# The second MLP product of a decoder layer, with the weight operands of two neighbouring sets side by side

## The chip, the cores and the metric

The kernel runs on one core of a Trainium2 chip. It is one launch that computes one layer of a decoder on 512 tokens. What counts is the device time of that launch in microseconds. The time before is 2219.13 us, the median of 3 runs (2218.69 to 2220.06).

The engines of the core go by short names: PE is the matrix engine, with the weight loads of its instructions listed apart as PEld; DVE, ACT and POOL are the vector, scalar and general engines; SP issues transfers. Transfers that SP issues are run by the hardware queue, those that POOL issues by the software queue, and both are carried by the same 16 DMA engines.

## What is computed

```python
def reference(x, w_in, conv_w, a_log, dt_bias, delta_norm_w, attn_sinks, rel_bias,
              w_o, ln1_g, ln1_b, w_up, w_down, ln2_g, ln2_b):
    for l in range(DEPTH):
        mixed = hybrid_mixer(x, w_in[l], conv_w[l], a_log[l], dt_bias[l], delta_norm_w[l],
                             attn_sinks[l], rel_bias, w_o[l])
        x = layer_norm(DN_ALPHA * x + mixed, ln1_g[l], ln1_b[l])
        x = layer_norm(DN_ALPHA * x + squared_relu_mlp(x, w_up[l], w_down[l]), ln2_g[l], ln2_b[l])
    return x

def squared_relu_mlp(h, w_up, w_down):
    a = jax.nn.relu(h @ w_up)
    return (a * a) @ w_down
```

`x` is 512 tokens by 2048, `w_up` 2048 by 8192, `w_down` 8192 by 2048, all float32. The mixer (a banded attention and a gated delta rule side by side) fills the first part of the launch and is not touched by the change. The change is in the last product, `(a * a) @ w_down`.

## The kernel before

**One product out of three.** A float32 operand is cut in two parts, hi and lo: ACT rounds it to the matrix format (hi), DVE subtracts that from the source (lo). A product of two operands is three matrix products summed in PSUM, hi by hi, hi by lo, lo by hi (`mul3`, line 105; `split`, line 109; their instructions stand under lines 107, 110 and 111).

**Seven products out of eight.** The last product is tiled in `g` (8 pieces of 1024 of the contraction) and `j` (4 pieces of 512 output columns). One `(g, j)` is a *set*. Within it, tokens, contraction and columns are each halved, and a scheme of seven products in place of eight is run: product `m` multiplies an operand of the activations (512 of the contraction by 256 tokens, sums of quarters, made by `Rows`) with an operand of the weights (512 of the contraction by 256 columns). The products come in the order `ORDER = (0, 3, 4, 6, 2, 1, 5)`. Results go to three PSUM banks per set, named in `PAIR`: products 0, 2, 1, 5 accumulate in bank "a", 3 in "e", 4 and 6 in "f". After every product DVE adds the bank, as it then stands, into a quarter of the output `y` (which lies in the tile `mix`; line 1002, called here the *evacuation*). So when one bank serves two products in a row, the second may not be written before DVE has read the first.

**The weights come by a chain.** The weight operand of most products is a sum of quarter blocks of `w_down` (512 KB each). The sums are made by transfers: a raw tile is loaded, cut for one product, and then a transfer issued by POOL adds the next block into the same raw tile in place (`accum_op=ALU.add`, line 186). A set has two such tiles. The tile x serves products 0, 4, 2 and 5, with an add after 0, after 4 and after 2. The tile y serves 3, 6 and 1, with a plain load after 3 (SP, line 188) and an add after 6. Before, `chained_pair` runs two neighbouring sets (`j` and `j + 1`) in turn: product `m` of the one, `m` of the other, then the next `m`. A chain of one tile therefore has four cuts from one use to the next.

**What sets the order.** `Stream` (line 113) holds the loads and the cuts in lists. Each `get()` hands out one cut operand and pumps: as far as room is free, loads and cuts are written into the program ahead. There are four slots for cut operands, so the cut that is written at a `get()` goes into the slot that the operand before has just left, and serves the operand three places further on. Each engine works its instructions strictly in the order in which they were laid down, and waits on semaphores of the others. `down` (line 1353) calls `get()`, then lays down 24 matmuls, then the evacuation.

**The activations' operands** of the next `g` are made meanwhile: `Rows` loads `hf` from memory (line 1293), sums quarters on DVE into `st` (line 1002) and cuts them into slots, one step after each of seven of the fourteen products (`steps`, line 1380).

## Time and profile before

| | |
|---|---|
| median of 3 runs | 2219.13 us (2218.69 to 2220.06) |
| the profiled execution's own time | 2220.53 us |
| its span, first to last instruction | 2218.7 us |
| mean granted clock of PE | 0.989 |
| PE busy | 2152.5 us of the span |
| DVE, ACT, POOL busy | 1461.3, 981.7, 327.5 us |
| the last product's stage | from about 1540 to 2208 us of the span |

The page gives busy times for the whole launch, and stages differ; the stage of the last product is read in windows of the trace, counted in microseconds from the span's start. A matmul is pipelined: its own length in the trace is longer than the distance to the next one, so the pace of a stage is its length divided by the number of matmuls in it. A row of the timeline or of a group of instructions names the line, the engine, the operation, the tile written and the tiles read, and then the idle time of that engine ahead of it with what ended that idle time.

### The profile page before, as it was taken

To read this page: it belongs to the slowest core of one execution; us is meant where nothing else is said; L and a number is where in the kernel's file an instruction comes from. 1 tells how busy PE (TensorE), PEld (TensorE's weight loads), DVE (VectorE), ACT (ScalarE), POOL (GpSimd) and SP (SyncE) were. 2 spreads that over 40 slices of the span, in tenths; PEclk is the share of its full clock that TensorE was granted. 3 is DMA by queue.
4 is the path that set the end of the run, shared out by engine and by line. 5 is a ranking of instruction groups with operands and counts; after the bars stand their busy time and mean duration, and the time that the engine had idled before them with its cause. 6 is when DMAs were issued, how large, how long until landed. Compare 5 with 4: busy or idle time off the path is not lost.

```text
span 2218.7 us, 37232 instructions
## 1 busy us (share of the span) xinstructions
PE 2152.5 (97%) x15051; PEld 1974.7 (89%) x15051; DVE 1461.3 (66%) x2170; ACT 981.7 (44%) x1474; POOL 327.5 (15%) x395
## 2 busy tenths in 40 slices
PE   8999999999999999899999999998999999999996
PEld 6777788788888887799999999998999999999995
DVE  3455667566654337867755565667778778778787
ACT  3244434334233224555555555555444444444442
POOL 0122020101100000321111211110111211112113
PEclk9999999999999999999999999999999999999998
DMA  7322341332324231499898898986788888888862
GB/s 208 95 72 81 96 116 58 98 87 69 98 64 170 90 122 46 136 206 232 212 210 216 207 219 208 207 202 225 178 219 215 195 212 216 203 211 213 204 146 93
DMA packets 164392, 352.63 MB, mean 159 GB/s; under 512 B 20123, under 2 KB 92236, under 8 KB 161660
## 3 DMA queue, kind: packets, MB, share of 16 engines
q0 software_dynamic: 38336, 130.08, 32.1%
q1 hardware_dynamic: 125884, 220.18, 29.5%
q8 instruction: 118, 1.93, 0.4%
q14 instruction: 54, 0.44, 0.1%
HBM read 325.01 MB, written 24.66 MB: 158 GB/s over the span
## 4 chain that ended last, share of the span: by engine, by line
PE 75%; issue 8%; DMA 7%; DVE 6%; ACT 2%; POOL 2%; SPq 0%; POOLq 0%; ACTq 0%; DVEq 0%
PE b L107 45%; PE pj L107 16%; PE po L107 8%; DMA raw<-in_w_down_dram 2%; DMA hf<-hd 2%; DVE lo L111 1%; DMA T<-in_w_down_dram 1%; PE ps_s L507 1%; ACT hi L110 1%; DVE mix L1439 1%; PE ps_o L554 1%; DMA g<-in_ln_dram 1%; DMA xc<-in_x_dram 1%; DMA C<-grow 1%; PE ps_pt L538 1%
## 5 line engine op out<-in xcount | busy, mean ns | idle before, releaser
L107 PE MATMUL b<-slot,hi 128*128 128x256 f32 x3584 | 646.7, 283 | 8.7 <-DVE slot L1041 3.3
L111 DVE TENSOR_TENSOR lo<-raw,hi 128x1024 fp32r<-128x1024 f32 x339 | 417.4, 1231 | 315.5 <-ACT hi L110 312.9
L110 ACT ACTIVATE hi<-raw 128x1024 fp32r<-128x1024 f32 x339 | 358.5, 1058 | 502.5 <-PE b L107 251.8
L107 PEld LDWEIGHTS b<-slot,hi 128*128 128x128 f32 x3584 | 555.5, 190 | 10.6 <-DVE slot L1041 4.1
L107 PE MATMUL b<-slot,lo 128*128 128x256 f32 x1792 | 507.3, 283 | 1.6 <-DVE lo L111 1.6
L107 PE MATMUL b<-hi,slot 128*128 128x256 f32 x2608 | 476.2, 282 | 9.6 <-ACT hi L110 9.6
L107 PE MATMUL pj<-slot,hi 128*128 128x512 f32 x1408 | 458.8, 403 | 0.0
L107 PEld LDWEIGHTS b<-hi,slot 128*128 128x128 f32 x2608 | 405.9, 189 | 10.6 <-ACT hi L110 10.6
L107 PE MATMUL b<-lo,slot 128*128 128x256 f32 x1304 | 368.0, 282 | 0.8 <-DVE lo L111 0.7
L107 PEld LDWEIGHTS b<-slot,lo 128*128 128x128 f32 x1792 | 340.2, 190 | 2.5 <-DVE lo L111 2.5
L107 PEld LDWEIGHTS pj<-slot,hi 128*128 128x128 f32 x1408 | 260.2, 189 | 60.6 <-issue 6.9
L107 PE MATMUL pj<-slot,lo 128*128 128x512 f32 x704 | 281.5, 400 | 1.0 <-DVE lo L111 1.0
L110 ACT ACTIVATE hi<-T 128x1024 fp32r<-128x1024 f32 x164 | 173.6, 1059 | 199.8 <-PE b L107 178.6
L111 DVE TENSOR_TENSOR lo<-T,hi 128x1024 fp32r<-128x1024 f32 x164 | 201.7, 1230 | 83.8 <-ACT hi L110 83.6
L107 PEld LDWEIGHTS b<-lo,slot 128*128 128x128 f32 x1304 | 246.3, 189 | 1.4 <-DVE lo L111 1.3
L1002 DVE TENSOR_TENSOR mix<-mix,b 128x512 f32<-128x512 f32 x223 | 152.0, 682 | 61.3 <-PE b L107 61.0
L107 PE MATMUL b<-hl,slot 128*128 128x256 f32 x1296 | 165.8, 284 | 4.8 <-DVE mix L1002 4.8
L107 PEld LDWEIGHTS b<-hl,slot 128*128 128x128 f32 x1296 | 160.0, 192 | 6.2 <-issue 4.3
L107 PEld LDWEIGHTS pj<-slot,lo 128*128 128x128 f32 x704 | 132.9, 189 | 30.4 <-DVE lo L111 1.9
L186 POOL DMA_DIRECT2D raw<-in_w_down_dram x90 | 77.7, 863 | 498.6 <-DVE lo L111 276.7
L1002 DVE TENSOR_TENSOR F<-F,b 128x512 f32<-128x512 f32 x144 | 98.9, 686 | 77.2 <-PE b L107 75.8
L107 PE MATMUL po<-hi,slot 128*128 128x512 f32 x448 | 140.7, 395 | 0.0
(263 smaller groups left out, 2118.9 us busy)
## 6 DMA issues: line engine op xcount, KB each, us to landing
raw<-in_w_down_dram POOLq DMA_DIRECT2D x90, 512.0 KB, 5.7
raw<-in_w_in_dram SPq DMA_DIRECT2D x88, 512.0 KB
raw<-in_w_up_dram POOLq DMA_DIRECT2D x84, 512.0 KB, 6.4
T<-in_w_down_dram SPq DMA_DIRECT2D x60, 512.0 KB
T<-in_w_up_dram SPq DMA_DIRECT2D x56, 512.0 KB
raw<-in_w_up_dram SPq DMA_DIRECT2D x44, 512.0 KB
raw<-in_w_down_dram SPq DMA_DIRECT2D x34, 512.0 KB
raw<-in_w_o_dram SPq DMA_DIRECT2D x32, 512.0 KB
```

The costliest lines, as they stand in the source:

```text
L107: nc.tensor.matmul(ps, a, b, start=first, stop=last, skip_group_check=more)
L110: nc.scalar.activation(hi, src, AF.Copy)
L111: nc.vector.tensor_tensor(out=lo, in0=src, in1=hi.bitcast(F32), op=ALU.subtract)
L186: nc.gpsimd.dma_start(src, nxt_, accum_op=ALU.add)
L507: nc.tensor.matmul(sc, qT[hp, b * P:(b + 1) * P], kd[hp, e, b * P + k0 - 128:(b + 1) * P], start=True, stop=True)
L538: nc.tensor.transpose(pst[:, (bb * 2 + kk) * P:(bb * 2 + kk + 1) * P], lg[a][:, b, kk * P:(kk + 1) * P], ident)
L554: nc.tensor.matmul(pso[a * 64:(a + 1) * 64, b * P:(b + n) * P], vt[:, b, vf_, vh:vh + 64], pTf[:, (2 * b + 1) * P:(2 * b + 1 + n) * P], st ...
L1002: eng.tensor_tensor(out=dst, in0=p, in1=q, op=op)
L1439: nc.vector.tensor_tensor(out=yt, in0=yt, in1=g, op=ALU.mult)
```

## The change

Two neighbouring sets are no longer run in turn but as one. A weight operand now holds the blocks of both sets side by side, so that one matmul has 512 columns. Since a slot for cut operands keeps its size, such an operand is given in two halves of the contraction (`kh` = 0 and 1, 256 each): two `get()`, each with 12 matmuls (2 tiles of 128 tokens, 2 steps of the contraction, 3 parts). A bank now holds one tile of 128 tokens by the 256 columns of both sets, and it is evacuated in the second half, once per tile of tokens (`t`).

The raw tiles of the chains are pairs: one tile holds the block of both sets. There are four pairs; those of the first stage's raw tiles are joined to two, one comes in the pool `fp2`, and one is the tile `F` of the first product once that has ended. The fourth slot for cut operands moves from `F` to `fp2` in turn. The next transfer of a chain is issued after the cut of the second half, as two transfers, one per block. The tiles `st` for sums of the activations become two halves of one fixed slot (`sums`), and the tile `T` becomes a slot for an activations' operand. The very last sets (`g` = 7, `j` = 2 and 3) keep their way.

The raw and cut tiles of the whole launch are now slices of one large tile each (`raws`, `cuts`); up to the last product, the order on each engine stays the same but for a few neighbours that change places.

```diff
--- before.py
+++ after.py
...
-            self.cut_free, self.used = deque(), []
-            self.room(pool, raws, cuts)
-            self.raw_free[tag].extend([(pool, raws)] * raws)
+            self.cut_free, self.used, self.kept = deque(), [], None
+            self.base = pool.tile([P, raws, 1024], F32, name="raws", bufs=1)
+            self.free["raw"].extend(self.base[:, j, :] for j in range(raws))
+            self.n_raw = raws
+            self.room(pool.tile([P, cuts, 2048], F32R, name="cuts", bufs=1))
+
+        def room(self, t):
+
+            self.cut_free.extend(t[:, j, :] for j in range(t.shape[1]))
...
         def load(self, tag):
-            live, loads, room = self.live[tag], self.loads[tag], self.raw_free[tag]
+            live, loads, free = self.live[tag], self.loads[tag], self.free[tag]
             while live and self.last[live[0][0]] < self.n_cut:
-                room.append(live.popleft()[1])
-            if not loads or not room or loads[0][2] > self.n_cut:
+                free.append(live.popleft()[1])
+            if not loads or loads[0][2] > self.n_cut:
+                return False
+
...
                 return False
             key, srcs, _ = loads.popleft()
-            a = srcs[0].shape[1]
-            pool, bufs = tok = room.popleft()
-            raw = pool.tile([P, a, 1024 // a], F32, tag=tag, name=tag, bufs=bufs)
-            n = 1024 // a // len(srcs)
-            for j, src in enumerate(srcs):
-                nc.sync.dma_start(raw[:, :, j * n:(j + 1) * n], src)
+            tok = free.popleft()
+            if tag == "W":
+                raw = tok
+                self.bring(raw, srcs)
+            else:
+                a = srcs[0].shape[1]
+                raw = tok.rearrange("p (a b) -> p a b", a=a)
+                n = 1024 // a // len(srcs)
+                for j, src in enumerate(srcs):
+                    nc.sync.dma_start(raw[:, :, j * n:(j + 1) * n], src)
             self.raws[key] = raw
             live.append((key, tok))
             return True
 
+        def bring(self, raw, srcs, add=False):
+
+            for n, src in enumerate(srcs):
+                if add:
+                    nc.gpsimd.dma_start(raw[:, n, :], src, accum_op=ALU.add)
+                else:
+                    nc.sync.dma_start(raw[:, n, :], src)
+
...
-            tok = None
             if dst is None:
-                pool, bufs = tok = self.cut_free.popleft()
-                if bufs:
-                    dst = [pool.tile(list(src.shape), F32R, tag=t, name=t, bufs=bufs) for t in ("hi", "lo")]
+                tok = self.cut_free.popleft()
+                if len(src.shape) == 4:
+                    v = tok.rearrange("p (h k n c) -> p h k n c", h=2, k=2, n=2)
+                    split(v[:, 0], v[:, 1], src)
+                    v = tok.rearrange("p (h k c) -> p h k c", h=2, k=2)
                 else:
-                    v = pool.tile([P, 2] + list(src.shape)[1:], F32R, tag="F", name="hl")
-                    dst = v[:, 0], v[:, 1]
-            split(*dst, src)
+                    v = tok.rearrange("p (h a b) -> p h a b", h=2, a=src.shape[1])
+                    split(v[:, 0], v[:, 1], src)
+                dst = v[:, 0], v[:, 1]
+            else:
+                split(*dst, src)
             if then:
                 what, nxt_ = then
-                if what == "add":
+                if isinstance(nxt_, tuple):
+                    self.bring(self.raws[keys[0]], nxt_, add=what == "add")
+                elif what == "add":
                     nc.gpsimd.dma_start(src, nxt_, accum_op=ALU.add)
                 else:
                     nc.sync.dma_start(src, nxt_)
...
+            while self.load("raw") or self.load("T") or self.load("W") or self.cut():
...
+    CHAIN = {0: ("add", (0, 1)), 4: ("add", (1, 1)), 2: ("add", (1, 0)), 3: ("load", (1, 1)), 6: ("add", (0, 1))}
...
         keys = [(ws.block(b(0, 0)), ws.block(b(1, 0), tag="T", gate=gate)) for b in blks]
         for m in ORDER:
             for (kx, ky), b in zip(keys, blks):
-                then = {0: ("add", (0, 1)), 4: ("add", (1, 1)), 2: ("add", (1, 0)),
-                        3: ("load", (1, 1)), 6: ("add", (0, 1))}.get(m)
+                then = CHAIN.get(m)
                 ws.add([ky if m in (3, 6, 1) else kx], then=then and (then[0], b(*then[1])))
+
+    def chained_wide(blks):
+
+        def both(i_, j):
+            return tuple(b(i_, j).rearrange("p k c -> p (k c)") for b in blks)
+
+        kx, ky = ws.block(*both(0, 0), tag="W"), ws.block(*both(1, 0), tag="W")
+        for m in ORDER:
+            for kh in range(2):
+                then = CHAIN.get(m) if kh else None
+                ws.add([ky if m in (3, 6, 1) else kx],
+                       lambda t, kh=kh: t.rearrange("p n (k c) -> p k n c", k=4)[:, 2 * kh:2 * kh + 2],
+                       then=then and (then[0], both(*then[1])))
...
-    tq = ctx.enter_context(tc.tile_pool(name="tq", bufs=NT))
-    ws.room(tq, NT, 0, tag="T")
+    tq = ctx.enter_context(tc.tile_pool(name="tq", bufs=1))
+    tqt = tq.tile([P, 2, 1024], F32, tag="T", name="tqt")
+    temps.append(tqt)
+    ws.free["T"].extend(tqt[:, j, :] for j in range(2))
...
     for g in range(ND):
         for j in (0, 2):
             if g < ND - 1 or j == 0:
-                chained_pair([down_block(g, j + n) for n in range(2)], gate=ws.n_op if g + j == 0 else 0)
+                chained_wide([down_block(g, j + n) for n in range(2)])
             else:
                 summed_set(down_block(g, j))
...
             split(v[:, 0], v[:, 1], src)
             self.ops[m] = v
-            self.toks[m] = pool
-
-        def sum(self, p, q, op=ALU.subtract):
-            out = fp2s["p"].tile([P, 4, 256], F32, tag="st", name="st", bufs=2)
+            self.toks[m] = tok
+
+        def sum(self, n, p, q, op=ALU.subtract):
+            out = sums[0][:, n]
...
-            ws.room(p, 2, 0)
-            free.extend([sb1] * 2 + [actp] * 8)
+            ws.room(p.tile([P, 1, 2048], F32R, name="cut4"))
+            ws.free["W"].append(p.tile([P, 2, 1024], F32, name="pair"))
+            sums.append(slot(sb1).bitcast(F32).rearrange("p (a k s) -> p a k s", a=2, k=4))
+            free.extend([sb1] + [actp] * 8)
...
-            ws.room(tq2, 0, 1)
+            ws.room(tq2.tile([P, 1, 2048], F32R, name="cut3"))
...
-    def down(g, js, order, table, rows, after):
-        banks = [{} for _ in js]
+    def down(j, w, order, table, rows, after):
+
+        banks = {}
+        yj = y[:, :, j * 512:(j + w) * 512].rearrange("p t (n c) -> p t n c", n=w)
         for m in order:
             key, *outs = table[m]
-            for j, bk in zip(js, banks):
-                first = key not in bk
-                if first:
-                    bk[key] = nb()
-                ps = bk[key]
+            first = key not in banks
+            if first:
+                banks[key] = [nb() for _ in range(w)]
+            op = rows.ops[m]
+            for kh in range(w):
                 hi, lo = ws.get()
-                op = rows.ops[m]
                 for t in range(2):
                     tok = slice(t * P, (t + 1) * P)
-                    for k in range(4):
-                        mul3(ps[:, t * 256:(t + 1) * 256], op[:, 0, k, tok], op[:, 1, k, tok],
-                             hi[:, k, :], lo[:, k, :], first and t == 0 and k == 0, t == 1 and k == 3,
-                             more=not first)
+                    ps, o = (banks[key][t], 0) if w == 2 else (banks[key][0], t * 256)
+                    for k in range(4 // w):
+                        kk = kh * 2 + k
+                        mul3(ps[:, o:o + w * 256], op[:, 0, kk, tok], op[:, 1, kk, tok], hi[:, k, :], lo[:, k, :],
+                             first and kk == 0 and o == 0, kk == 3 and (w == 2 or t == 1), more=not first)
+                    if w == 2 and kh:
+                        for row, col, sign in outs:
+                            v = yj[:, 2 * row + t, :, col * 256:(col + 1) * 256]
+                            sub(nc.vector, v, v, ps.rearrange("p (n c) -> p n c", n=2),
+                                ALU.add if sign > 0 else ALU.subtract)
+            if w == 1:
                 for row, col, sign in outs:
-                    v = y[:, 2 * row:2 * row + 2, j * 512 + col * 256:j * 512 + (col + 1) * 256]
+                    v = yj[:, 2 * row:2 * row + 2, 0, col * 256:(col + 1) * 256]
                     sub(nc.vector, v, v, ps.rearrange("p (t c) -> p t c", t=2),
                         ALU.add if sign > 0 else ALU.subtract)
             after(m)
...
-    ws.cut_free.append((fp, 0))
+    F2 = hold["F"].rearrange("p f s -> p (f s)")
+    ws.kept = F2.rearrange("p (n c) -> p n c", n=2)
+    ws.free["W"].append(ws.kept)
+    temps.append(ws.kept)
+    free.append(tq.tile([P, 2048], F32R, tag="T", name="slot"))
...
         for j in (0, 2):
-            down(g, (j, j + 1), ORDER, PAIR, rows, after)
+            down(j, 2, ORDER, PAIR, rows, after)
         rows = new
...
+    for j0, w, order, table in ((0, 2, ORDER, PAIR), (2, 1, range(7), LONE)):
+        down(j0, w, order, table, rows, lambda m: None)
...
-    g2 = [tq.tile([P, 2, 512], F32, tag="T", name="g2", bufs=NT) for _ in range(2)]
-    g2 += [fp2s["p"].tile([P, 2, 512], F32, tag="st", name="g2", bufs=2) for _ in range(2)]
+    g2 = [ws.kept[:, n].rearrange("p (a s) -> p a s", a=2) for n in range(2)]
+    g2 += [sums[0][:, n].rearrange("p k s -> p (k s)").rearrange("p (a s) -> p a s", a=2) for n in range(2)]
```

Three places show how the order on the engines moves. The first is DVE in a pair of sets, around the evacuation of product 4, before the change. `raw` and `T` are the x and y tiles of the chains, `lo` and `hl` cut operands, and the banks 19987 and 20018 are "f" of the two sets.

```order
L1002 TENSOR_TENSOR mix_83<-mix_83,b_19957 128x2x256
L111 TENSOR_TENSOR lo_19989<-T_19683,hi_19988 128x1024
L1002 TENSOR_TENSOR mix_83<-mix_83,b_19987 128x2x256
L111 TENSOR_TENSOR lo_20020<-raw_18827,hi_20019 128x1024
L1002 TENSOR_TENSOR mix_83<-mix_83,b_20018 128x2x256
L111 TENSOR_TENSOR lo_20055<-raw_18858,hi_20054 128x1024
```

Cuts and evacuations alternate. The evacuation of the first set's product 4 (bank 19987) stands ahead of the cut of that set's product 2 (from `raw_18827`).

The same place after the change. `pair` is the x tile of this pair of sets, `raws` its y tile, `cut3`, `cut4` and `cuts` are the slots, and 14214 and 14215 are bank "f" of the two tiles of tokens.

```order
L110 TENSOR_TENSOR cut4_13404<-raws_87,cut4_13404 128x1024
L110 TENSOR_TENSOR cut3_7405<-pair_13405,cut3_7405 128x1024
L1062 TENSOR_TENSOR mix_83<-mix_83,b_14214 128x2x256
L1062 TENSOR_TENSOR mix_83<-mix_83,b_14215 128x2x256
L110 TENSOR_TENSOR cuts_88<-pair_13405,cuts_88 128x1024
L110 TENSOR_TENSOR cuts_88<-raws_87,cuts_88 128x1024
L1062 TENSOR_TENSOR mix_83<-mix_83,b_14214 128x2x256
L1062 TENSOR_TENSOR mix_83<-mix_83,b_14215 128x2x256
```

Now come two cuts, two evacuations, two cuts, two evacuations. The second row is the first half of product 2's operand, cut from the x tile, and both evacuations of product 4 stand behind it. The fifth row is its second half.

The third place is PE after the change, over products 4, 6 and 2 of the same pair of sets: `cut3`, `cut4` and `cuts` are weight operands, the last name in a row is the activations' operand.

```order
L106 MATMUL b_14214<-cut3_7405,slot_13651 128x512 x6
L106 MATMUL b_14215<-cut3_7405,slot_13651 128x512 x6
L106 MATMUL b_14214<-cuts_88,slot_13651 128x512 x6
L106 MATMUL b_14215<-cuts_88,slot_13651 128x512 x6
L106 MATMUL b_14146<-cut3_7405,slot_13971 128x512 x2
L106 MATMUL b_14214<-cuts_88,slot_13933 128x512 x6
L106 MATMUL b_14215<-cuts_88,slot_13933 128x512 x6
L106 MATMUL b_14214<-cut4_13404,slot_13933 128x512 x6
```

The first four rows are product 4, the last three product 6 in the same banks. Two matmuls of product 2 (bank 14146, the half operand of the DVE row above) are put between them. In the other pair of sets of a `g` nothing stands between. Before, 24 matmuls of the other set lay between two uses of one bank.

More of the change, by code (lines that the diff above doesn't have):

```diff
@@ L193, in pump @@
         def pump(self):
-            while self.load("raw") or self.load("T") or self.cut():
+            while self.load("raw") or self.load("T") or self.load("W") or self.cut():
                 pass
         def get(self, n=1):
-            self.cut_free.extend(t for t in self.used if t)
+            self.cut_free.extend(t for t in self.used if t is not None)
             self.used = []
@@ L880, in hymba_layer, with temp @@
         chains.append(delta(pr, st))
+    temps = []
     def summed_set(blk, first=False, pool=()):
         t_ = {}
+        def temp():
+            t = temps[-1]
+            return [t[:, j].rearrange("p (k c) -> p k c", k=4) for j in range(2)]
         def plus(name, p, q, out=None):
             if out is None:
-                out = tq.tile([P, 4, 256], F32, tag="T", name="T", bufs=NT)
+                out = temp()[("t1", "t2").index(name)]
             eng = nc.gpsimd if name in pool else nc.vector
@@ L1282, in hymba_layer, with free_slot @@
     fp2s = {}
-    free = deque()
+    free, sums = deque(), []
+    def free_slot():
+        tok = free.popleft()
+        return tok, slot(tok) if tok in (sb1, actp) else tok
     def quads(f0, f1):
@@ L1320, in make @@
                 self.cut(4, self.s1)
[L1321 removed]
+                self.s1 = self.sum(0, self.s2, a12, ALU.add)
             elif m == 6:
                 self.cut(6, self.s1)
[L1324 removed]
+                self.s1 = self.sum(0, a11, a21)
             else:
@@ L1399, in res_slot @@
         if free:
-            t = slot(free.popleft())
+            t = free_slot()[1]
         else:
```

42 lines of the change are left out of this document (25 added, 17 removed).

## The prediction

> **What bounds the kernel now.** First the page's parts 1 and 2, then windows of the span with each engine's busy time in them.
>
> ```profile
> span 2218.7 us, 37232 instructions
> PE 2152.5 (97%) x15051; PEld 1974.7 (89%) x15051; DVE 1461.3 (66%) x2170; ACT 981.7 (44%) x1474; POOL 327.5 (15%) x395
> ...
> core 0: us, PE busy (x) PEld busy (x) DVE busy (x) ACT busy (x) POOL busy (x), PEclk, DMA share, GB/s
> 700.00:780.00 80.00, 80.00 (x345) 64.84 (x345) 27.90 (x31) 16.98 (x17) 0.00 (x0) 1.00 0.33 106
> 1620.00:2060.00 440.00, 436.76 (x3665) 435.72 (x3664) 349.74 (x366) 198.13 (x191) 76.00 (x88) 1.00 0.86 209
> 1800.00:1840.00 40.00, 40.00 (x339) 40.00 (x338) 27.96 (x31) 15.57 (x15) 7.11 (x9) 1.00 0.84 187
> ```
>
> PE bounds the launch (97%), and the stage that changes too: in the second window, which lies wholly in the last product, it is busy for 436.76 of 440 us at a granted clock of 1.00. A matmul of 256 columns there takes 440/3665 = 120.05 ns with all idle time in it, 436.76/3665 = 119.2 ns without, and 40/339 = 118.0 ns in a stretch with none; I take 118.6 for its own pace. The first window is another stage, whose matmuls all have 512 columns: 80/345 = 231.9 ns each. The DMA engines come next, 0.86 of their time.
>
> How near is the rest to PE? The waits in the second window (engine, line, what it waited for; microseconds in all, times, the longest):
>
> ```profile
> PE b L107 <- DVE mix L1002: 3.2, 6, 0.8
> ...
> ACT hi L110 <- PE b L107: 131.4, 81, 1.8
> ...
> ACT hi L110 <- DMA T<-in_w_down_dram: 9.0, 5, 2.5
> ```
>
> PE waited six times for an evacuation, 3.2 us in all. ACT, which begins each cut, waits for PE to leave a slot and hardly ever for a transfer. So the chains of adds are in time now, and PE's pace is what remains.
>
> **What the change gives PE.** It removes 336 matmuls of 256 columns per pair of sets (2 sets, 7 products, 24 each) and puts 168 of 512 columns there. Fifteen of the sixteen pairs change, 2520 matmuls: 2 x 118.6 - 231.9 = 5.3 ns each, 13 us in all (10 to 16 by the two ends 118.0 and 119.2). A pair would take 168 x 0.2319 = 38.96 us in place of 336 x 0.12005 = 40.34. Cuts, transfers, bytes, the elements of the evacuations and the sums of the activations stay the same in number; the part before 1540 us keeps its order. I cost these at nothing.
>
> The Trainium skill (TensorE: Matmul & The Clock Gate, Back-to-back issue gap) gives N/2.4 + 2.5 ns at the full clock, so 109.2 and 215.8 ns: an estimate of 2.5 ns per exchange, 6 us in all. Both rows here are slower than that, and the difference between them is larger; the sum goes by the rows.
>
> **What it does to the chain of adds.** This decides. The parts of one link, from the timeline of a stretch, two rows of DVE working without a pause, and the chain of waits:
>
> ```profile
> 1649.46 1.22 DVE L111 TENSOR_TENSOR lo<-raw,hi 128x1024 fp32r<-128x1024 f32 x1 [0.41 <-ACT hi L110]
> 1650.98 0.86 POOL L186 DMA_DIRECT2D raw<-in_w_down_dram  x1 [1.98 <-DVE lo L111]
> 1651.03 0.28 PE L107 MATMUL b<-hi,slot 128*128 128x256 f32 x1
> 1651.23 1.06 ACT L110 ACTIVATE hl<-T 128x1024 fp32r<-128x1024 f32 x1 [1.81 <-PE b L107]
> 1652.33 1.23 DVE L111 TENSOR_TENSOR hl<-T,hl 128x1024 fp32r<-128x1024 f32 x1 [0.41 <-ACT hl L110]
> ```
> ```profile
> 1714.16 1.21 DVE L111 TENSOR_TENSOR lo<-T,hi 128x1024 fp32r<-128x1024 f32 x1
> 1715.29 1.22 DVE L111 TENSOR_TENSOR slot<-st,slot 128x1024 fp32r<-128x1024 f32 x1
> 1716.43 0.68 DVE L1002 TENSOR_TENSOR mix<-mix,b 128x512 f32<-128x512 f32 x1
> 1717.03 1.22 DVE L111 TENSOR_TENSOR lo<-raw,hi 128x1024 fp32r<-128x1024 f32 x1
> ```
> ```profile
> 1683.53 8.92 DMA T<-in_w_down_dram
> ...
> 1692.56 1.07 ACT hi L110
> ...
> 1705.04 0.61 DVE mix L1002
> 1705.64 0.14 issue
> 1705.78 14.27 PE b L107 x118
> ```
>
> A slot left by PE is taken by ACT 0.20 us later (1651.03 to 1651.23), DVE's half of the cut begins 1.10 after ACT's (1651.23 to 1652.33) and ends after 1.22, POOL issues 0.30 after that end (1650.68 to 1650.98). On DVE cuts follow each other in 1.13, an evacuation takes 0.60 more. A landed transfer is cut from 0.11 on (1692.45 to 1692.56), and PE goes on 0.14 after an evacuation.
>
> Now the transfers: queues, the groups of issues with their size and median landing, and one line's landings.
>
> ```profile
> q0 software_dynamic: 12672, 46.14, 57.5%
> q1 hardware_dynamic: 10958, 45.46, 28.1%
> ...
> raw<-in_w_down_dram POOLq DMA_DIRECT2D x66, 512.0 KB, 5.7
> ...
> T<-in_w_down_dram POOLq DMA_DIRECT2D x22, 512.0 KB, 7.4
> ...
> DMA to landing us min/median/max: 5.1/6.1/9.4
> ```
>
> The 88 adds hold all 16 engines for 57.5% of 440 us, 2.875 us each, twice the time per byte of the plain loads (28.1% of 440 us for as many bytes, on q1). Before, an add is issued after each cut, and cuts of one chain come 24 matmuls, 2.85 us, apart: the queue has just carried one add when the next is issued. After, the cut of `kh` = 0 issues nothing and that of `kh` = 1 issues two, 0.86 apart. The second can't land before 5.1 + 2.875 = 7.98 us: call that time, from the first issue to both landed, L. And since a half of the contraction of product 2 is cut from both blocks, its first cut waits for both.
>
> The trace can't show what such a pair of adds takes. Bounds for L: 5.1 + 0.86 = 5.96 if they don't hinder each other; 6.1 + 2.875 = 9.0 from the median landing. I take 7.98, since four of the adds' engine times (57.5%) already fill most of the queue.
>
> That cut now stands on DVE ahead of the evacuation of the product before (the second order above). Where the next product uses the same bank (4 then 6, 2 then 1, 1 then 5), PE waits for that evacuation, thus for L. So the chain closes on itself, once per pair of sets. From the end of one product 1 to the end of the next:
>
> - the second cut of product 0: 0.20 + 1.10 + 1.22 = 2.52; issue 0.30; L
> - product 4's first cut, half an evacuation pair, second cut: 0.11 + 1.10 + 1.13 + 0.60 + 1.22 = 4.16; 0.30; L
> - product 2's first cut, both evacuations of 4, second cut: 0.11 + 1.10 + 1.13 + 1.20 + 1.22 = 4.76; 0.30; L
> - product 5's first cut, the first evacuation of 2, PE: 0.11 + 1.10 + 1.13 + 0.68 + 0.14 = 3.16
> - product 1 itself, 24 x 0.2319 = 5.57.
>
> The sum is 21.07 + 3 L. With L = 7.98 it is 45.0 us, against 38.96 that PE alone needs and 40.34 now: 4.66 more per pair than now. PE stands for 45.0 - 39.0 = 6 us in each pair, ahead of products 6 and 1. What waits behind the cut on DVE besides (sums and cuts of activations for the next `g`) has slack of several products. The first pair starts with slots and raw tiles loaded, so 14 of 15 are paced so: 14 x 4.66 = 65 us. The first is worth 1.4 less, which I leave out. On the profiled execution (span 2218.7, its own time 2220.5, median of the runs 2219.1) I put it on the median: 2219 + 65 = 2284 us.
>
> The break-even is 21.07 + 3 L = 40.34, L = 6.42. With L = 6.75 the sum gives 2219 + 14 x 0.98 = 2233; with L = 9.0, 48.1 per pair, 2219 + 14 x 7.7 = 2327.
>
> **The rivals.**
>
> *A: the adds overlap, the chain closes in time, and the 512 columns pay.* It wants L below 21.07 + 3 L = 38.96, L = 5.96, exactly the bound of adds that don't hinder each other. For it: the two write different parts, and DMA engines are idle 14% of the time. Against it: 2.875 us of all sixteen for each. It would give 2219 - 13 = 2206; with short waits of 0.5 us at three places in 15 pairs, 2215 to 2219. This is the faster side: 0.09.
>
> The Trainium skill (DMA: Bandwidth & Descriptors, Anatomy of one DMA — SWDGE (gpsimd) path) fits such a transfer as 2.0 us + bytes/436e3, an estimate of 3.2 us for one add and 4.4 for two behind each other. By that rule L is 4.4, the chain closes with time to spare, and rival A holds. The trace disagrees: 5.1 us is the fastest landing of one add, and 2.875 us the engines' time of each, so I give it no more than A's chance.
>
> *B: L as long as the usual landing.* The stage's other loads (q1, 28.1%) come between the adds. L = 9.0 or more, 2327 and up. For it: y tiles' adds land in 7.4 at the median now. Against it: a longer stage spreads the same bytes, so the queue is emptier. 0.13.
>
> *C: gain and wait cancel.* L between 6.2 and 6.6: 2215 to 2223. 0.06.
>
> *D: the pairs of tiles do not let a chain start early.* If product 0's raw pair (two plain loads) arrived late, PE would stand between sets. There are four pairs and two in use, so loads come a pair of sets ahead; this adds nothing unless it also stalls. It is in the upper end of the range.
>
> **How the numbers follow.** The forecast (the chain, L from 6.7 to 8.9) has 0.72; A 0.09, B 0.13, C 0.06. The time is that of the forecast, 2284. The range reaches from 2232 to 2330: below lie A, C and a short L, above the worse half of B. A measurement here tells 0.2% (4.4 us) from no change: faster 0.09, same 0.06, slower 0.85.
>
> **What would show it.** In the profile after: PE's waits for evacuations rise from 3.2 us in 440 to several us per pair of sets, at the starts of products 6 and 1; ACT's `hi` waits for transfers instead of PE; POOL's issues come in twos, 0.86 apart, and both land after 8 us; the share of q0 falls; between the stalls a matmul still takes 232 ns. It would be wrong if the pairs of adds land within 6.4 us of the first issue, if PE is busy throughout, or if the stalls stand elsewhere (at product 0 for raw tiles, or in the stage before 1540 us).

## The result, and the profile after

The changed kernel takes 2329.99 us, the median of 4 runs (2324.67 to 2336.29), against 2218.91 before (here the median of 4 runs). The ratio is 1.0491, with a 95% interval of 1.0471 to 1.0512: slower by 111 us. The forecast was slower by 65, with a range up to 2330: the median lies 0.01 us below that end, and two of the four runs lie above it. One of the ten executions of E4 below took 5092.45 us and is left out of its times.

The page's first lines and, in the order of the forecast, the same window of the last product's stage as before, with the same columns. The profiled execution is 6 us longer than the median.

```profile
span 2334.4 us, 32070 instructions
PE 2186.0 (94%) x12531; PEld 1873.5 (80%) x12531; DVE 1449.7 (62%) x2170; ACT 977.9 (42%) x1474; POOL 329.3 (14%) x395
...
1620.00:2060.00 440.00, 384.47 (x1536) 301.87 (x1537) 289.86 (x310) 166.28 (x163) 65.02 (x74) 0.92 0.73 177
```

PE idles for 55.5 of 440 us where it had idled for 3. A pair of sets has 168 matmuls, so 1536 of them are 9.14 pairs, and a pair takes 440/9.14 = 48.1 us where the forecast had 45.0 and the kernel before 40.3. One column was in no term of the forecast: the granted clock, 0.92 in place of 1.00.

What PE and ACT waited for in that window (microseconds in all, times, the longest):

```profile
PE b L106 <- DVE mix L1062: 37.5, 15, 6.3
...
ACT cuts L109 <- DMA raws<-in_w_down_dram: 78.1, 18, 9.8
...
ACT cut L109 <- DMA pair<-in_w_down_dram: 43.5, 11, 7.3
...
PE b L106 <- ACT cut L109: 13.4, 5, 3.9
```

ACT's cuts wait for the adds (78.1 and 43.5 us), and PE waits for evacuations (37.5 us) and for the late cut itself (13.4 us). The loop can be read off the chain of waits, from the add after product 0 on (start, length, what; the pieces of some hundredths of a microsecond left out):

```profile
1742.68 0.54 POOL pair L190
1743.22 7.39 DMA pair<-in_w_down_dram
...
1750.71 1.07 ACT cut L109
...
1751.81 1.23 DVE cut L110
1753.03 0.99 DVE mix L1062 x2
...
1754.14 1.23 DVE cuts L110
...
1755.66 0.46 POOL pair L190
...
1756.20 7.21 DMA pair<-in_w_down_dram
...
1763.52 1.06 ACT cut L109
...
1764.60 1.24 DVE cut L110
...
1765.88 8.92 PE b L106 x25
```

Two adds, 0.54 apart, land 0.54 + 7.39 = 7.93 us after the first issue. The next two after 7.75 (1755.66 to 1763.41). Cut, evacuations, cut and the next issue follow as in the forecast's links, but for one: between the two cuts behind the first landing stand two evacuations, where the forecast had one. Then comes PE with 25 matmuls in 8.92 us, 0.36 us each, and that is the clock. The timeline of the place (PE, and a window around it):

```profile
1764.62 0.51 PE L106 MATMUL b<-cut,slot 128*128 128x512 f32 x1 [2.45 <-ACT cut L109]
1765.88 0.79 PE L106 MATMUL b<-cut,slot 128*128 128x512 f32 x1 [0.75 <-DVE cut L110]
1766.48 5.49 PE L106 MATMUL b<-cuts,slot 128*128 128x512 f32 x12
...
1776.96 2.97 PE L106 MATMUL b<-cuts,slot 128*128 128x512 f32 x12
```
```profile
1764.00:1772.00 8.00, 6.62 (x15) 4.88 (x16) 3.56 (x4) 1.52 (x2) 1.75 (x2) 0.57 0.80 146
```

After a wait of 2.45 us, one matmul and a wait of 0.75 us, PE works at about half speed for some 6 us: 12 matmuls in 5.49 us, where ten microseconds later 12 take 2.97. The mean granted clock of these 8 us, 0.57, says the same.

In this pair of sets the slow PE is itself a piece of the chain. The adds after product 2 are issued at 1768.45 and have landed at 1776.37, but ACT begins the cut that they serve (for product 5) only at 1777.15, because cuts ahead of it had waited for PE. So PE's lateness costs the loop 0.8 us here, not the 3 us by which its 25 matmuls are slow.

Last, POOL's issues of adds: the first of the stage, two pairs of sets, and the first of the last pair that the change touches:

```profile
1546.16 0.86 POOL L190 DMA_DIRECT2D pair<-in_w_down_dram  x1 [60.30 <-DVE cuts L110]
...
1742.68 1.76 POOL L190 DMA_DIRECT2D pair<-in_w_down_dram  x2 [16.86 <-DVE cuts L110]
1755.66 1.76 POOL L190 DMA_DIRECT2D pair<-in_w_down_dram  x2 [11.22 <-DVE cuts L110]
1760.26 1.75 POOL L190 DMA_DIRECT2D raws<-in_w_down_dram  x2 [2.84 <-DVE cut L110]
1768.45 1.75 POOL L190 DMA_DIRECT2D pair<-in_w_down_dram  x2 [6.44 <-DVE cuts L110]
1788.66 1.76 POOL L190 DMA_DIRECT2D raws<-in_w_down_dram  x2 [18.45 <-DVE cut L110]
1802.47 1.76 POOL L190 DMA_DIRECT2D raws<-in_w_down_dram  x2 [12.05 <-DVE cut L110]
...
1818.94 1.76 POOL L190 DMA_DIRECT2D raws<-in_w_down_dram  x2 [8.99 <-DVE cut L110]
1838.10 1.75 POOL L190 DMA_DIRECT2D pair<-in_w_down_dram  x2 [17.40 <-DVE cuts L110]
...
2220.77 1.76 POOL L190 DMA_DIRECT2D pair<-in_w_down_dram  x2 [22.24 <-DVE cuts L110]
```

Each pair of sets has four issues: x after 0, x after 4, y after 6, x after 2. In the first pair of a `g` the x tile is `pair` and the y tile `raws`, in the second the x tile is `raws` and the y tile `F`, whose row is left out here. From the first x issue to the next pair's, the first pair of this `g` takes 1788.66 - 1742.68 = 46.0 us, the second 1838.10 - 1788.66 = 49.4, and so it alternates through the stage. (Fourteen pairs, from 1546.16 to 2220.77, take 674.6 us, 48.2 each.) The second is longer at its adds after product 4 (1802.47 to 1818.94, 16.5 us, where the first pair has 12.8). Beside them runs a load of `hf`, 1 MB, issued 0.9 us behind:

```profile
1803.33 21.77 SPq L1357 DMA_DIRECT2D hf<-hd  x2
```
```profile
DMA to landing us min/median/max: 6.3/8.3/10.4
```

The first line is SP's queue (two loads, the first at 1803.33). The second is of the two adds issued at 1802.47 and 1803.00: the one landed after 6.3 us, the other after 10.4, which is 10.9 us after the first issue. The link before it, after product 0, is longer than in the first pair too. In the chain, behind the first cut:

```profile
1798.70 1.19 DVE mix L1062 x2
1799.90 1.14 DVE slot L110
```

Beside the two evacuations a cut of an activations' operand (tile `slot`), 1.14 us, stands ahead of the second cut and with it ahead of the issue at 1802.47.

### The profile page after: what moved, and what is told of

Read it like the earlier page. It is cut to its first block, busy times and chain, and to the rows that moved or that the text cites. A ratio compares the mean times of both kernels' runs of the same rounds, so it can differ in the third digit from the quotient of the medians.

```text
span 2334.4 us, 32070 instructions
## 1 busy us (share of the span) xinstructions
PE 2186.0 (94%) x12531; PEld 1873.5 (80%) x12531; DVE 1449.7 (62%) x2170; ACT 977.9 (42%) x1474; POOL 329.3 (14%) x395
## 4 chain that ended last, share of the span: by engine, by line
PE 65%; DMA 13%; DVE 10%; issue 6%; ACT 3%; POOL 2%; SPq 0%; ACTq 0%; POOLq 0%; DVEq 0%
PE b L106 32%; PE pj L106 18%; PE po L106 8%; DMA raws<-in_w_down_dram 6%; DMA pair<-in_w_down_dram 5%; DVE cut L110 2%; DVE cuts L110 2%; DVE mix L1062 1%; ACT cut L109 1%; ACT cuts L109 1%; DVE slot L110 1%; POOL raws L190 1%; PE ps_s L544 1%; PE ps_z L795 1%; PE ps_c L805 1%
## 5 line engine op out<-in xcount | busy, mean ns | idle before, releaser
L110 DVE TENSOR_TENSOR cuts<-raws,cuts 128x1024 fp32r<-128x1024 f32 x255 | 315.0, 1235 | 391.7 <-ACT cuts L109 390.6
L106 PE MATMUL pj<-slot,cuts 128*128 128x512 f32 x2112 | 532.5, 402 | 0.8 <-DVE cuts L110 0.8
L109 ACT ACTIVATE cuts<-raws 128x1024 fp32r<-128x1024 f32 x255 | 270.0, 1059 | 526.9 <-PE b L106 176.2
L106 PE MATMUL b<-slot,cuts 128*128 128x256 f32 x3672 | 462.7, 286 | 7.4 <-DVE slot L1101 3.5
L106 PEld LDWEIGHTS pj<-slot,cuts 128*128 128x128 f32 x2112 | 389.2, 189 | 90.8 <-issue 6.9
L106 PEld LDWEIGHTS b<-slot,cuts 128*128 128x128 f32 x3672 | 452.7, 192 | 9.6 <-DVE slot L1101 4.3
L106 PE MATMUL b<-cut,slot 128*128 128x512 f32 (+1 forms) x1356 | 340.7, 402 | 88.5 <-DVE mix L1062 53.0
L106 PEld LDWEIGHTS b<-cut,slot 128*128 128x128 f32 x1356 | 255.4, 195 | 159.6 <-DVE mix L1062 52.9
L106 PE MATMUL b<-cuts,slot 128*128 128x512 f32 (+1 forms) x1332 | 336.6, 406 | 9.1 <-DVE mix L1062 6.9
L106 PEld LDWEIGHTS b<-cuts,slot 128*128 128x128 f32 x1332 | 259.3, 199 | 76.1 <-issue 7.7
```

The costliest lines, as they stand in the source:

```text
L106: nc.tensor.matmul(ps, a, b, start=first, stop=last, skip_group_check=more)
L109: nc.scalar.activation(hi, src, AF.Copy)
L110: nc.vector.tensor_tensor(out=lo, in0=src, in1=hi.bitcast(F32), op=ALU.subtract)
```

## Experiments

E1 to E11 are changes of the changed kernel unless another is named. Times are medians, beside the kernel before on the same chip (2220.3, 2219.8 and 2220.3 in the three groups E1 to E4, E5 to E8, E9 to E11).

**E1: the evacuations ahead of the cut that waits.** The cut is laid down after the second evacuation, and tied to stand behind it on DVE (`late` hands an operand out without laying down a cut, `last` is the evacuation of `t` = 1).

```diff
-                hi, lo = ws.get()
+                hi, lo = ws.get(late=w == 2 and kh == 1)
...
+            if w == 2:
+                with tc.issue_after(last.ins):
+                    ws.pump()
```

> The changed kernel with one thing moved: on DVE both evacuations of product m stand ahead of the first cut of product m+2, which waits for the two adds. Adds, matmuls and bytes stay. Theory 1 (the loop closes because PE waits for an evacuation that is queued behind a cut that waits for the adds): with the evacuation ahead, the adds have until PE reaches product m+2 itself; by the links of the prediction (2.52 + 0.30 + 8 = 10.8 us after the end of product 1, PE ends product 0 at 11.1) every link is in time, PE paces the stage, and the time is 2219 - 13 = 2206, up to 2225 with some short waits. Theory 2 (two adds at once are too late for PE whatever stands on DVE): 2290 to 2330 as before. Theory 3 (the half clock after a stall keeps itself up): still over 2250.

Measured: 2280.63 us (2275.31 to 2287.66), ratio 1.0275 (1.0247 to 1.0303). The window of the stage:

```profile
1620.00:2060.00 440.00, 409.31 (x1679) 322.21 (x1678) 313.47 (x335) 176.34 (x176) 69.65 (x80) 0.97 0.78 191
```

Half the loss is gone (49 of 111 us) and the other half is not, so the first theory's number is missed by far, and the second's too. Only the third's (over 2250, by the clock) fits, and E5 tests that one. The order on DVE is a part of the cause and not the whole.

**E2: the adds by halves of the contraction.** Each cut is followed by two adds of 256 KB, in place of two of 512 KB after the second cut.

```diff
-                then = CHAIN.get(m) if kh else None
+                then = CHAIN.get(m)
+                if then and then[0] == "load" and not kh:
+                    then = None
...
-                       then=then and (then[0], both(*then[1])))
+                       then=then and ("add%d" % kh if then[0] == "add" else "load", both(*then[1])))
...
+                        c = slice(int(what[3]) * 512, int(what[3]) * 512 + 512)
+                        self.bring(self.raws[keys[0]][:, :, c], [a[:, c] for a in nxt_], add=True)
```

> The changed kernel with the adds split by the half of the contraction: after each cut (kh = 0 and kh = 1) two adds of 256 KB, in place of two of 512 KB after the second cut. DVE's rule for cut and evacuation stays. Theory 1: the first half's adds start one half product (2.8 us) earlier and need half the engine time, 5.1 to 6.5 us in all; the loop is then 31 to 36 us against PE's 39, so PE paces: 2206 to 2225. Theory 2 (the queue is the limit, whatever the pieces; small transfers cost more): 2290 or more.

Measured: 2234.74 us (2225.61 to 2240.59), ratio 1.0066 (1.0042 to 1.0089). The window, its waits of PE, and two groups of issues (KB each, median to landing):

```profile
1620.00:2060.00 440.00, 426.26 (x1806) 340.36 (x1805) 342.64 (x363) 196.46 (x189) 148.17 (x169) 0.99 0.90 207
```
```profile
PE b L106 <- DVE mix L1068: 13.7, 11, 2.8
```
```profile
raws<-in_w_down_dram POOLq DMA_DIRECT2D x82, 256.0 KB, 5.8
...
pair<-in_w_down_dram POOLq DMA_DIRECT2D x67, 256.0 KB, 5.5
```

With the adds in time, 95 of the 111 us are gone, though the cut still stands ahead of the evacuation on DVE, the bytes are the same, and the queue of the adds is no cheaper (60.8% of the window for 44.79 MB, where the changed kernel has 49.6% for 40.01 MB). The run doesn't separate the earlier issue of the first half from the smaller size. The time is 10 us above the expected range. What remains are waits for evacuations, 13.7 us of 440, up to 2.8 us each.

**E3: both.** The edits are those of E1 and E2.

> E1 and E2 together. If either closes the loop, this adds nothing over the better one: 2206 to 2215. If both only shorten it, this is faster than each by several us.

Measured: 2233.49 us (2231.08 to 2238.09), ratio 1.0063 (1.0048 to 1.0079), the same as E2. Once the adds are in time, the order of cut and evacuation is worth nothing more. The expected range, up to 2215, is missed by 18 us, as E2's is by 10.

**E4: plain loads in place of the adds.** The table of the chains is changed, so the adds of the first MLP product go too.

```diff
-    CHAIN = {0: ("add", (0, 1)), 4: ("add", (1, 1)), 2: ("add", (1, 0)), 3: ("load", (1, 1)), 6: ("add", (0, 1))}
+    CHAIN = {0: ("load", (0, 1)), 4: ("load", (1, 1)), 2: ("load", (1, 0)), 3: ("load", (1, 1)), 6: ("load", (0, 1))}
```

> The changed kernel with every accumulating add replaced by a plain load of the same block on SP's queue (the sums of weight blocks are left out, bytes from memory and order of the rest stay). Theory 1: two plain loads land in 5 us in place of 8 (1.4 us of engines each in place of 2.9), the loop is 21 + 3 x 5 = 36 us, below PE's 39: 2206 to 2215, no stalls, granted clock 1.00 in the stage. A rival by which the wider matmuls or the joined evacuations themselves are slower: 2260 or more.

Measured: 2217.54 us (2209.04 to 2223.49), ratio 0.9986 (0.9969 to 1.0003), just above the expected 2206 to 2215.

```profile
1620.00:2060.00 440.00, 432.81 (x1849) 344.42 (x1849) 342.74 (x366) 196.50 (x189) 0.00 (x0) 1.00 0.58 208
```

The long waits go with the adds. But the time only comes back to that of the kernel before: 7 us of 440 are still lost to short waits, 5.1 of them for evacuations:

```profile
PE b L106 <- DVE mix L1062: 5.1, 10, 1.6
```

Some 5 us of what is won lie ahead of the stage, with the adds of the first MLP product: the first load of `hf` is issued at 1505.6 us of the span, and at 1511.0 in the kernel before.

**E5: more work for PE, at the place where it waits.**

```diff
+            if w == 2 and m == 4:
+                for u in range(18):
+                    nc.tensor.matmul(banks["e"][u % 2], op[:, 0, 0, 0:P], hi[:, 0, :], start=True, stop=True)
```

> The changed kernel with 18 more matmuls of 512 columns in each of the 15 pairs of sets, laid down behind product 4, at the place where PE stands. They write the bank of product 3 once that is evacuated, and nobody reads them. They are 15 x 18 x 0.232 = 63 us of work for PE. Theory 1 (the loop of adds paces the stage; PE only waits, and the half clock after its waits costs little by itself): the time stays at 2330, or falls by up to 15 where the fuller PE keeps its clock. Theory 2 (the half clock after a stall is what makes the stage 46 us longer than forecast): with no long stalls the clock stays at 1.00 and the time falls to 2290 or less. Theory 3 (PE's own work paces): 2330 + 63 = 2390.

Measured: 2331.85 us (2330.34 to 2333.07), against 2329.99 without.

```profile
1620.00:2060.00 440.00, 410.18 (x1710) 326.02 (x1709) 289.40 (x310) 166.17 (x162) 64.94 (x74) 0.97 0.73 177
```

63 us of matmuls cost 2 us. A pair now has 186, so 1710 are 9.19 pairs in 440 us: 47.9 us each, as before (48.1), with the clock at 0.97 in place of 0.92. The run changes two things at once, more work and a fuller clock, and shows their sum: the time doesn't follow PE's work, and it doesn't fall as the clock rises, which the second theory wanted.

**E6: the load of `hf` later.**

```diff
+            e = ws.last_sub
...
+            if (j, m) == (2, 6):
+                with tc.issue_after(e.ins):
+                    nc.vector.tensor_copy(small.tile([P, 1], F32, tag="tn", name="keep"), new.f[0][:, 0, 0:1])
```

> The changed kernel with the first of the two activations' loads of each g (hf, 1 MB) held back until after product 6 of the second pair, by an element of its tile that is read there, so that it no longer runs beside the pair of adds after product 4. Theory 1 (that load makes these adds land after 10.9 us and not 7.9, and all of it goes into the loop): seven times 3 us less, 2330 - 21 = 2309, and the pair of adds lands in 8. Rival (the loop has slack there, or the load only moves the collision to the next adds): 2325 to 2335.

Measured: 2311.11 us (2308.04 to 2322.99), ratio 1.0419 (1.0391 to 1.0447): 19 us less than the changed kernel, 21 expected. POOL's issues in a second pair of sets, from its first to the next pair's first:

```profile
1778.34 1.75 POOL L190 DMA_DIRECT2D raws<-in_w_down_dram  x2 [17.72 <-DVE cut L110]
1792.22 1.75 POOL L190 DMA_DIRECT2D raws<-in_w_down_dram  x2 [12.12 <-DVE cut L110]
...
1805.58 1.75 POOL L190 DMA_DIRECT2D raws<-in_w_down_dram  x2 [5.88 <-DVE cut L110]
1823.47 1.75 POOL L190 DMA_DIRECT2D pair<-in_w_down_dram  x2 [16.13 <-DVE cuts L110]
```

From the adds after product 4 to those after 2 it is now 1805.58 - 1792.22 = 13.4 us and not 16.5, and the pair takes 45.1 and not 49.4. The adds after product 4 have landed 7.8 us after their first issue, where the changed kernel's took 10.9.

**E7: E4 with 256 columns.** Each matmul of 512 columns is run as two of 256 in the same bank; the sums are left out as in E4.

```diff
+                        for n in range(w):
+                            c, d = slice(o + n * 256, o + n * 256 + 256), slice(n * 256, n * 256 + 256)
+                            mul3(ps[:, c], op[:, 0, kk, tok], op[:, 1, kk, tok], hi[:, k, d], lo[:, k, d],
...
```

> E4 (plain loads in place of the adds, the sums left out) with each matmul of 512 columns run as two of 256. Nothing else moves. Against E4 it shows what the width is worth where PE paces: the prediction's 2 x 118.6 - 231.9 = 5.3 ns in 2520 places, 13 us more than E4, so 2231. If the pace of the stage is set by something else (waits for evacuations, cuts), the same as E4 within 4 us.

Measured: 2230.17 us (2225.71 to 2240.30), ratio 1.0053 (1.0036 to 1.0070): 13 us over E4, 13 expected. PE idles for 3.9 of 440 us in its window and for 7.2 in E4's, so the difference is not the width alone.

**E8: a version meant to be fast.** E2's halves, E6's late load, both halves of an operand taken at once and the tiles of tokens as the outer loop, the cuts behind the last evacuation.

```diff
-            for kh in range(w):
-                hi, lo = ws.get()
-                for t in range(2):
+                hl = ws.get2()
+                for t in range(2):
+                    for kh in range(2):
+                        hi, lo = hl[kh]
...
+                with tc.issue_after(last.ins):
+                    ws.free2()
```

> A version meant to be fast: the halves of E2, the late load of E6, the tiles of tokens as the outer loop (12 matmuls of one tile of tokens over both halves of the contraction, then 12 of the other) so that 12 matmuls and not 6 lie between the end of a bank and its next use, and the cuts behind the last evacuation as in E1. E2 and E3 stand some 30 us of stalls above E4, of them 20 in the first pair of sets and 1.5 to 3 us once or twice per g. If these latter are what the evacuations miss by, they vanish: 2212 to 2222. If the later release of the slots makes the cuts late: over 2235.

Measured: 2214.53 us (2213.04 to 2219.84), ratio 0.9973 (0.9960 to 0.9986): faster than the kernel before, by 5 us.

```profile
1620.00:2060.00 440.00, 439.38 (x1888) 353.49 (x1887) 351.12 (x383) 204.82 (x198) 155.38 (x176) 1.00 0.94 217
```

In the steady part PE waits no more (0.6 us of 440): 440/1888 = 233.1 ns per matmul, 39.2 us per pair. What is not won yet lies at the stage's start, where PE is busy for 66 us of the 80 from 1540 to 1620, and for 71 in the kernel before:

```profile
1540.00:1620.00 80.00, 66.15 (x259) 51.41 (x260) 53.99 (x58) 31.97 (x34) 25.43 (x29) 0.89 0.84 188
```
```profile
1540.00:1620.00 80.00, 71.44 (x565) 70.19 (x564) 59.54 (x63) 33.25 (x33) 12.98 (x15) 0.94 0.86 204
```

(E8 above, the kernel before below.)

**E9: E1 with E6's late load.** The two edits are those shown.

> E1 (evacuations ahead of the waiting cut) with the late load of E6. E1 came out at 2281, not at 2206: its first pairs of a g take 40 to 42 us, its second pairs, in which the load of hf runs beside the adds after product 4 (10.9 us to landing), 47 to 49. Theory (that load is what keeps E1's loop open in the second pairs): without it they take 40 to 42 too, seven times 7 us less, about 2230. Rival (E1's second pairs are long for the cuts and sums of activations that stand on DVE): about 2265 to 2280.

Measured: 2271.33 us (2268.06 to 2274.67), ratio 1.0215 (1.0173 to 1.0256). The rival's range holds. A second pair of sets in it and the first pair behind it, by POOL's first issues:

```profile
1764.08 1.75 POOL L190 DMA_DIRECT2D raws<-in_w_down_dram  x2 [17.39 <-DVE cut L110]
...
1806.17 1.75 POOL L190 DMA_DIRECT2D pair<-in_w_down_dram  x2 [14.88 <-DVE cuts L110]
...
1851.66 1.75 POOL L190 DMA_DIRECT2D raws<-in_w_down_dram  x2 [18.60 <-DVE cut L110]
```

The second pair takes 42.1 us, where E1's took 47 to 49. But the whole time fell by 9 us, not by the 35 that this makes over seven `g`: the first pairs lost most of it, 45.5 us in these rows (1806.17 to 1851.66), where E1's took 39 to 42. Why they became longer is not settled. With whole adds and without the load the pairs still take 42 to 46 us, above PE's 39.

**E10: 256 columns in the changed kernel itself.** E7's edit, adds kept.

> The changed kernel with every matmul of 512 columns run as two of 256, the order, the adds and the evacuations left as they are. If the loop of adds paces the stage, PE's pace counts only in the one product of 24 matmuls that lies in the loop: 2330 + 14 x 24 x 0.0053 = 2332, the same within 5 us. If PE's work counts wherever it stands: 2343.

Measured: 2362.86 us (2361.83 to 2364.51), ratio 1.0627 (1.0593 to 1.0662): 33 us over the changed kernel, which neither theory had. It isn't the width alone that moved: the order on DVE came out otherwise too. In the changed kernel's chain above, two evacuations and nothing else stand between the cuts at 1751.81 and 1754.14. The same place in E10:

```profile
1755.24 1.23 DVE L110 TENSOR_TENSOR cut<-pair,cut 128x1024 fp32r<-128x1024 f32 x1 [3.13 <-ACT cut L109]
1756.38 0.68 DVE L1062 TENSOR_TENSOR mix<-mix,b 128x512 f32<-128x512 f32 x1
1756.98 1.22 DVE L1062 TENSOR_TENSOR slot<-slot,hf 128x1024 f32<-128x1024 f32 x1
1758.12 0.68 DVE L1062 TENSOR_TENSOR mix<-mix,b 128x512 f32<-128x512 f32 x1
...
```

A sum of activations (1.14 us) now stands in the loop. That is one link of several; how much of the 33 us is order and how much is width stays open, so this run decides nothing on the width.

**E11: E8 with the first pair's load later.** The activations' load for the next `g` waits for product 0's evacuation there.

```diff
+            if g == 0 and (j, m) == (0, 0):
+                with tc.issue_after(ws.last_sub.ins):
+                    nc.vector.tensor_copy(small.tile([P, 1], F32, tag="tn", name="keep0"), rows.f[0][:, 0, 0:1])
+                new = Rows(1)
```

> E8 with one more load moved: in the first pair of sets the activations' load for the next g waits until product 0's evacuation, so that the first adds don't share the engines with it. E8 has 7.2 us of waiting and then 5.9 us in that pair. If the load is what delays the first adds (they land after 12 to 14 us): 3 to 5 us less than E8's 2214.5. If the wait is for the writes of the first product's results, or moves to the next products: 2212 to 2220.

Measured: 2216.74 us (2214.32 to 2223.79), ratio 0.9980 (0.9962 to 0.9998). No gain over E8, as the second expectation had it. What holds up the first pair of sets is not settled.

## Why the prediction was right, and where it was short

**The number**: inside the range by 0.01 us, and that is luck. The loss of 111 us is 46 more than the forecast's 65. What decided, the loop of adds, was forecast; its length was not, and 48.1 us per pair is the figure that rival B had.

**What PE gains** (13 us): right in size. E7 against E4 gives 13, where PE sets the pace and waits differ by 3 us of 440.

**The loop of adds is what decides**: right. E5 adds 63 us of work for PE and the time doesn't move; E2 leaves the work and brings the adds in time, and 95 of 111 us go; E4 takes the adds away, and the long waits go. E2's pieces for the tiles `pair` and `raws` land in 5.5 and 5.8 us at the median, and the first of them start earlier.

**L = 7.98**: right where nothing else runs, 7.93 and 7.75 in the chain quoted. Wrong in one of the six x links of a `g`: in the second pair, beside `hf`, two adds take 10.9 us. Rival B had this mechanism (other loads between the adds) but put it on every link; it is one load, and E6, which moves it, gives back 19 us.

**21.07 + 3 L per pair**: short. The fourteen pairs take 674.6 us where the sum gives 14 x 45.0 = 630, so 45 of the 46 us between 2284 and 2330 lie in them. The first pairs take 46.0 where the sum has 45.0, the second 49.4; the stage's first pair (1546.16 to 1597.65) takes 51.5. Three terms of the sum were too small.

- "L" for all links alike: the link beside `hf` has 10.9 and not 8, some 3 us in each second pair, and E6 gives 19 us of it back.
- "half an evacuation pair", 0.60, between product 4's two cuts: the chain has both evacuations there, and from cut to cut it is 2.33 us (1751.81 to 1754.14) where the sum has 1.13 + 0.60.
- the sentence that sums and cuts of activations on DVE have slack: in the second pair's chain one such cut costs its full 1.14 us.

In the first pair PE's lateness, 0.8 us, comes to these, and the other landings are a little shorter than 7.98.

**PE stands 6.0 us per pair**: 55.5/9.14 = 6.1 by the window, and the agreement is luck. The loop is 3.1 us longer than forecast, and PE's own work filled just that: at the lower clock it is busy for 384.47/9.14 = 42.1 us per pair where the forecast had 39.0. The place is not quite the one I gave either: in the timeline quoted PE waits for product 2's cut itself (two of its matmuls are laid ahead of product 6), and behind that wait it runs slowly, so that it comes late to product 1 as well. I read this as the reason why little is waited for there; no run tested it.

**The signs**: PE's waits for evacuations, ACT's waits for transfers and the falling share of q0 (57.5% to 49.6%) came as forecast. The two adds start 0.54 us apart and not 0.86, and a matmul between the stalls does not always take 232 ns.

**The clock** was missing altogether. The trace of before has it in the stage's first 80 us (0.94, in the row above), and I didn't read it there. It made little difference to the sum: by the chain 0.8 us in a first pair, an estimate of 5 us over seven `g`, and in E5, where fuller work lifts it from 0.92 to 0.97, the time stays. Mostly a slower PE uses up what would otherwise be waiting, since the adds set the pace. The Trainium skill (TensorE: Matmul & The Clock Gate, Part 1: The HAM clock gate) has PE fall to half its clock after an idle window of some 3.4 us. The trace agrees on the half (12 matmuls in 5.49 us against 2.97) and here shows it after a wait of 2.45 us, one matmul and 0.75 us more. Where PE sets the pace again behind such a wait, this would count.

**Rival A**: fell, since two adds took 7.93 and not under 5.96 us. The Trainium skill (DMA: Bandwidth & Descriptors, Anatomy of one DMA — SWDGE (gpsimd) path) fits a transfer as 2.0 us + bytes/436e3, by which my estimate for two was 4.4 us. The trace disagrees: these accumulating transfers took 7.93.

**Against the expectations of the runs**: E1 showed that my single cause for the loop (the evacuation behind the waiting cut) is half of it. In E1 PE still waits 22.7 us of 440 for evacuations and 7.3 for cuts, in E9 13.9 and 20.5. I read this as whole adds coming late for PE itself, since the cut begins only once PE has finished a whole product; no run separates it. E9 shows that it doesn't hang on `hf` alone. E2 needs no change of order because its first half is issued half a product earlier and lands sooner.

## What to carry to other kernels

Where transfers are chained to the work through a buffer that they update in place, count the loop (cut, issue, landing, next cut) against the engine's own time per round, with the landing of all transfers that are issued together; of the two issued at 1742.68 and 1743.22 one landed 5.4 us and the other 7.9 us after the first issue. Halving the piece, so that its first half is issued earlier, was worth 95 us here where moving the order was worth 49. Read for each link which other load runs beside it: one load of 1 MB, in one link of six, cost 19 us. On an engine that is not the bound, adding work where it waits (E5) tells in one run whether the time follows its work.

## What was not expected of the hardware

- After a wait of 2.45 us, one matmul and a wait of 0.75 us, PE's granted clock is near half for about 6 us (0.57 over 8 us): 12 matmuls of 512 columns take 5.49 us in place of 2.97.
- Two adds that POOL issues back to back start 0.54 us apart (1742.68 and 1743.22 in the chain), not the 0.86 of a single issue.
- Beside a load of 1 MB two adds took 10.9 us in place of 7.6 to 9.0 in the other x links of the steady pairs; with the load moved (E6) they took 7.8.
